# Four edits to the schedule of a hybrid encoder layer: output rows split one at a time, wider value copies, later linear attention groups, the second gate tile before the last norm

## The chip, the cores and the metric

The kernel runs on one core of a Trainium2 chip. The metric is device time in microseconds (us) of one execution, lower is better; the time given for a kernel is the median of its runs.

## What is computed

One layer of a streaming encoder, in float32, on 1024 tokens of width 1024. Cut to what matters:

```
h = rmsnorm(x, ln1);  z = h @ w_in            # columns: pool 256, gla q/k/v/g 4 x 256, gate rank 16,
                                              #          fox q/k/v 3 x 512, forget 8
y_pool = pool_mixer(u)                        # trailing means over 2, 4, 8, 16 tokens, minus identity, per-group linear
y_gla  = gla_mixer(q, k, v, g, a)             # chunked gated linear attention, 4 heads of 64, chunks of 64:
    bcum = cumsum(log_sigmoid(a @ w_a_up + b_a) / 16)            # the decays
    S_t = dec * S_{t-1} + k_in^T v;  o = causal(q k^T) v + q S   # within a chunk, and from the state
    o = rmsnorm(o) * gla_gn * silu(g)
y_fox  = fox_mixer(q, k, v, f)                # causal softmax(q k^T / 8 + F_t - F_s) v, 8 heads of 64,
                                              #   F = cumsum(log_sigmoid(f + b_f))
x = x + concat(y_pool, y_gla, y_fox) @ w_o
h = rmsnorm(x, ln2)
x = x + (silu(h @ w_gate) * (h @ w_up)) @ w_down                 # 22 tiles of 128 hidden columns
out = rmsnorm(x, ln_f)
```

## The kernel before

Every large matmul is done in three: both operands are split into a high part, rounded to TensorE's fp32r format by ScalarE, and a low part, the difference (VectorE or GpSimd), and high x high, high x low and low x high are added in PSUM (`gemm`, `woven`, L139 to L155).

**Memory.** On-chip memory is a set of slots of 128 x 1024 floats. `G` (L50) takes the slot that has been free longest (first in, first out) and `free` gives it back; `R` (L60) takes slots in turn from a small ring: `w` holds split weights (4 slots), `wr` raw weights (2), `p` attention scores (6), `pp` (3), `fb` (2). A tile's first write waits until all that read or wrote the slot's last owner are done, DMAs included. PSUM has eight banks in four groups (L27): `s` 3, `pt` 2, `o` 1, `gm` 2.

**Order.** The program is one straight list of instructions. A planner with a simulated timeline lays out each engine's order when the kernel is built: among what it believes ready it takes what stands first in the program, and it fills gaps with later work, however far down the program. On the chip each engine then follows its list strictly, and waits at an instruction whose inputs or slot are not there. All loads and stores but four go through SP's queue, which waits in order too.

**Stages**, with their rough place in the profile:

- Norm and transposes of x, the gate-rank and linear attention value projection (to 56 us).
- `decays` (L302): logits of the decays, log-sigmoid and running sums for both groups j of two linear attention heads, and for the forget gates F (stored to `Fd`).
- `pool_in`, then the linear attention groups `A = Gla(0)` and `B = Gla(1)` (L660 to L674). Each group has three projections (`keys`, `queries`, `gates`), and small pieces of TensorE work are woven into the projections' matmuls as `smalls`: `turn_keys` (tile pk), `state` (pkv), `within` (pat), `outputs` (po), `turned` (pot), and the pool's matmul (py). What has finished is split into high and low and stored by `keep_mix` (L270) to `mixs`.
- `fox_values(0)` (L517): values of the first two head pairs, eight token blocks, tile psv; each block is copied out as a high and a low part for each of two pairs, four instructions. Its tiles `v` hold one pair and four token blocks each. The last smalls of group B are woven in here.
- `keep_wo` (L279), eight times: a row block of the output weights is loaded, split and stored to `wod`, through three `G` slots.
- Four head pairs: `fox_qk(p)` (tiles zq, zk) and `fox_attend(p)` (L627; scores s, transposes pt, outputs o), which begins with the load of its bias rows `fb` from `Fd`. The values of the last two pairs are made after pair 1. At the end of each pair its tiles are freed (L684 to L695).
- Output projection in two halves of the contraction: `pxa` with row blocks 0 to 3 (L698 to L707), `pxb` with 4 to 7 (L934 to L951), each over eight token blocks; `fetch_wo` and `load_mix` bring the parts back from memory. After `pxb` of a block follows its second norm, `norm2` (L717; transposes n2pt in `pt`).
- SwiGLU, 22 gate tiles: seven products each in the place of eight (`gate_up`, L764, tile m; products are numbered 1 to 7 and come in the order 3, 5, 4, 1, 2, 7, 6, each 12 matmuls). `left` makes left operands hA from the transposed norm, `right`/`make` right operands wr from the weights. Products 3 and 5 need tokens 0 to 511 alone. Then the down projection the same way (tile d), and the last norm.

Around the last block of `pxb`, the first gate tile's first two products are started ahead of the norm:

```python
        if tb == NT - 1:
            for _ in range(2):
                next(first[0])
        SP.dma_start(x3d[tb], xs[tb])
        norm2(tb, xs[tb])
        free(f"xa{tb}")
    free(*[f"wo{k}{h}" for k in range(4, 8) for h in "hl"], "ln2b", *[f"mix{k}_1" for k in range(4, 8)])
    first.append(start(1))
    makes[1](3, 5)
    for _ in range(2):
        next(first[1])
```

The second gate tile is `start(1)`; product 3 goes to a bank of `s`, product 5 to one of `pt`.

Of the kernel before, what the change touches and what calls it, by code (L numbers as in the profile page):

```python
# [10 lines left out]
F32R = mybir.dt.float32r  # L11
I8 = mybir.dt.int8
AF = mybir.ActivationFunctionType
ALU = mybir.AluOpType
# [17 lines left out]
def tile_hybrid_block(ctx: ExitStack, tc, x, w_fv, w_gv, w_zt, w_o, w_gu, w_down, ln, w_pool, w_a3, chans, b_f, consts, out):  # L32
# [36 lines left out]
    def f(ap):  # L69
        return ap.bitcast(F32)  # L70
# [208 lines left out]
    def keep_wo(k):  # L279

        hi, lo = load_g(w_o[k * P:(k + 1) * P, :], f"wos{k}", tag="G")
        SP.dma_start(wod[k, :, 0], f(hi))
        SP.dma_start(wod[k, :, 1], f(lo))
        free(f"wos{k}h", f"wos{k}l")
# [15 lines left out]
    bcs = []  # L300

    def decays():  # L302

        las = []
        for j in range(2):
            la = R(f"la{j}")
            for c in range(2):
                csl = slice(c * 512, c * 512 + 512)
                ps = PS("s", f"pla{j}_{c}")
                PE.matmul(ps, wa[:, j * P:(j + 1) * P], aT[0:48, csl], start=True, stop=True)  # L310
                DVE.tensor_scalar(out=la[:, csl], in0=ps, scalar1=ch[:, 2 + j:3 + j], scalar2=None, op0=ALU.add)
            las.append(la)
        lft = R("lft")
        log_sigmoid([(la, la, R(f"lat{j}", tag="pp")) for j, la in enumerate(las)] + [(fx[0:8], fx[0:8], lft[0:8])])
        for j, la in enumerate(las):
            bc = G(f"bc{j}")
            DVE.tensor_tensor_scan(out=bc, data0=reset, data1=la, initial=0.0, op0=ALU.mult, op1=ALU.add)
            bcs.append(bc)
        ones, Fc = R("ones"), R("Fc")
        DVE.memset(ones[0:8], 1.0)  # L320
        DVE.tensor_tensor_scan(out=Fc[0:8], data0=ones[0:8], data1=fx[0:8], initial=0.0, op0=ALU.mult, op1=ALU.add)
        SP.dma_start(Fd, Fc[0:8])
        free("fx")
# [193 lines left out]
    def fox_values(q, smalls=((),) * NT):  # L517

        V = [[G(f"v{2 * q + j}_{i}", F32R).rearrange("p (t h s e) -> p t h s e", t=4, h=2, s=2) for i in range(2)] for j in range(2)]
        ws = [load_w(w_fv[:, q, i * 1024:(i + 1) * 1024], f"wfv{q}_{i}", eng=POOL) for i in range(2)]  # L520
        for tb in range(NT):
# [3 lines left out]
            for j in range(2):  # L525
                v_ = V[j][tb // 4][:, tb % 4]
                pv = ps[:, 128 * j:128 * j + 128].rearrange("p (h e) -> p h e", h=2)
                ACT.activation(v_[:, :, 0], pv, AF.Copy)
                DVE.tensor_tensor(out=v_[:, :, 1], in0=pv, in1=f(v_[:, :, 0]), op=ALU.subtract)
# [19 lines left out]
    def fox_item(p, a, m, ops, fb, V, Y):  # L549
# [44 lines left out]
        for n in range(m + 1):  # L594
# [10 lines left out]
            for b in range(2):  # L605
                kb = 2 * n + b
                o0 = cut * b
                v_ = V[p % 2][kb // 4][:, kb % 4, a]
# [51 lines left out]
    decays()  # L660
    free("aT", "reset", "wa")
# [3 lines left out]
    A.queries(((), A.turn_keys()))  # L665
    pools = pool_tile(1, us[1]), pool_tile(0, us[0])
    A.gates((A.state(), pools[0] + A.within(0)))
    B = Gla(1)
    B.keys((A.within(1) + A.outputs(0), A.outputs(1) + A.turned(0)))
    B.queries((A.turned(1) + pools[1], B.turn_keys()))  # L670
    free("misc")
    B.gates((B.state(), B.within(0)))
    o_ = [B.outputs(0), B.outputs(1)]
    V = fox_values(0, (B.within(1), o_[0][:1], o_[0][1:], o_[1][:1], o_[1][1:] + B.turned(0), B.turned(1), (), ()))  # L674
    for k in range(8):
        keep_wo(k)
    ops = fox_qk(0)
    free("gv0", "gv1", "attb0", "attb1")
    for p in range(4):
# [4 lines left out]
        done = [f"{n}{p}_{a}" for n in ("q", "k", "kl") for a in range(2)] + [f"v{p}_{i}" for i in range(2)]  # L684
        if p == 1:
            V = fox_values(1)
            free(*[done.pop() for _ in range(2)])
# [248 lines left out]
    for tb in range(NT):  # L936
# [9 lines left out]
        if tb == NT - 1:  # L946
            for _ in range(2):
                next(first[0])
# [3 lines left out]
    free(*[f"wo{k}{h}" for k in range(4, 8) for h in "hl"], "ln2b", *[f"mix{k}_1" for k in range(4, 8)])  # L952
    first.append(start(1))
    makes[1](3, 5)
    for _ in range(2):
        next(first[1])
# [166 lines left out]
```

## Time and profile before

| | us |
|---|---|
| median of 3 runs | 1177.58 (1176.51 to 1179.23) |
| profiled execution | 1175.42 |
| its span, first to last instruction | 1173.7 |
| TensorE matmul busy | 1136.0 |
| VectorE busy | 828.2 |
| ScalarE busy | 536.0 |
| GpSimd busy | 340.4 |

Times in the profile are from the span's start. PE is TensorE's matmuls, PEld its weight loads, DVE VectorE, ACT ScalarE, POOL GpSimd, SP the queue that issues DMAs; a name with q is an engine's queue. A row of a timeline has the start, the busy time, engine, line, operation, tile written and tiles read, form and count, and in brackets the idle time ahead of it and what ended that. A row of the waits has who waited for whom, the sum in us, how often, and the longest. A row of windows has the stretch, its length, each engine's busy time with its count, TensorE's granted clock (1.00 is full speed), the share of the DMA engines and GB/s. Matmuls are pipelined, so the busy time of one overlaps the next.

### The profile page before, as it was taken

The numbers are of one execution on the slowest core, as the hardware profiler recorded it, in microseconds if no ns is written. First come the engines' busy times: TensorE is split into PE (matmuls) and PEld (weight loads), VectorE is DVE, ScalarE is ACT, GpSimd is POOL, SyncE is SP. The second block draws the span as 40 slices with busy tenths as digits, with TensorE's granted clock in tenths as the row PEclk, the third lists the DMA queues.
The fourth block names the chain that finished last, engine by engine and source line by source line (L and its number), as shares of the span: only waits on it lengthen the run. The fifth ranks groups of instructions, "written<-read, shape, count | busy, mean of one in ns | idle before, by whom it ended". The sixth has DMA issues, their size and how long they took to land.

```text
span 1173.7 us, 15953 instructions
## 1 busy us (share of the span) xinstructions
PE 1136.0 (97%) x5928; PEld 958.5 (82%) x5928; DVE 828.2 (71%) x1365; ACT 536.0 (46%) x970; POOL 340.4 (29%) x260
## 2 busy tenths in 40 slices
PE   6999998999999999998999999999999999999996
PEld 5877878889978888886888888888888888888875
DVE  6697364387746866579997767767686685876686
ACT  6454233466654644456453433444344344334345
POOL 2231123343322413210302221022201370660784
PEclk9999999999999999999999999999999999999999
DMA  7121184411203734431323332242314688333233
GB/s 250 37 73 52 59 295 174 176 39 35 91 18 126 305 132 159 173 112 46 117 86 129 101 115 88 101 134 82 135 54 152 224 322 293 103 95 102 86 112 143
DMA packets 57692, 150.45 MB, mean 128 GB/s; under 512 B 5080, under 2 KB 5512, under 8 KB 57616
## 3 DMA queue, kind: packets, MB, share of 16 engines
q1 hardware_dynamic: 57184, 147.87, 36.5%
q0 software_dynamic: 432, 1.57, 0.4%
q8 instruction: 46, 0.75, 0.3%
q14 instruction: 30, 0.25, 0.1%
HBM read 105.09 MB, written 44.34 MB: 127 GB/s over the span
## 4 chain that ended last, share of the span: by engine, by line
PE 76%; DVE 4%; DMA 1%; issue 1%; POOL 1%; ACT 1%; SPq 0%; POOLq 0%; DVEq 0%; ACTq 0%
PE m L774 36%; PE d L1030 15%; PE pxa L144 4%; PE pxb L144 3%; PE o L615 3%; PE pt L601 2%; PE psv L152 2%; PE s L575 1%; PE s L576 1%; PE zq3p L152 1%; PE zq0p L152 1%; PE zq2p L152 1%; PE zk1p L152 1%; PE zk2p L152 1%; PE zk0p L152 1%
## 5 line engine op out<-in xcount | busy, mean ns | idle before, releaser
L774 PE MATMUL m<-hA_0h,wr 128*128 128x512 f32 x616 | 214.7, 391 | 1.2 <-ACT hr L729 1.2
L774 PE MATMUL m<-hA_1h,wr 128*128 128x512 f32 x616 | 214.9, 389 | 0.0
L774 PEld LDWEIGHTS m<-hA_0h,wr 128*128 128x128 f32 x616 | 116.1, 189 | 25.8 <-ACT hr L729 1.6
L774 PEld LDWEIGHTS m<-hA_1h,wr 128*128 128x128 f32 x616 | 115.8, 188 | 24.2
L1030 PE MATMUL d<-lw,ha 128*128 128x512 f32 x308 | 119.9, 389 | 0.9 <-DVE lw L880 0.9
L774 PE MATMUL m<-hA_0l,wr 128*128 128x512 f32 x308 | 120.3, 391 | 0.0
L774 PE MATMUL m<-hA_1l,wr 128*128 128x512 f32 x308 | 119.9, 389 | 0.0
L1030 PE MATMUL d<-hw,ha 128*128 128x512 f32 x308 | 119.3, 389 | 0.0
L1030 PE MATMUL d<-hw,la 128*128 128x512 f32 x308 | 118.4, 389 | 0.0
L756 ACT ACTIVATE wr<-ws 128x512 fp32r<-128x512 f32 x110 | 69.5, 632 | 101.5 <-DVE ws L755 50.1
L826 POOL TENSOR_TENSOR cg<-cu,cu 128x512 f32<-128x512 f32 x11 | 19.7, 1795 | 302.8 <-DVE cu L803 266.7
L757 DVE TENSOR_TENSOR wr<-ws,wr 128x512 fp32r<-128x512 f32 x110 | 76.8, 704 | 20.6 <-ACT wr L756 20.5
L880 DVE TENSOR_TENSOR la<-ra,ha 128x1024 fp32r<-128x1024 f32 (+1 forms) x42 | 57.2, 1368 | 32.0 <-ACT ha L879 24.7
L590 POOL TENSOR_TENSOR pb<-pb,rl 128x128 f32<-128x128 f32 (+3 forms) x32 | 39.0, 1222 | 117.5 <-DVE rl L587 108.9
L872 POOL TENSOR_TENSOR rw<-wd,wd 128x512 f32<-128x512 f32 x33 | 59.0, 1815 | 47.7 <-PE d L1030 47.6
L879 ACT ACTIVATE ha<-ra 128x1024 fp32r<-128x1024 f32 (+1 forms) x42 | 41.3, 987 | 65.6 <-DMA ra<-cd 56.8
L1030 PEld LDWEIGHTS d<-lw,ha 128*128 128x128 f32 x308 | 57.8, 188 | 13.3 <-DVE lw L880 1.3
L604 DVE TENSOR_TENSOR pp<-pt,pp 128x512 fp32r<-128x512 f32 (+1 forms) x80 | 50.2, 631 | 25.7 <-ACT pp L603 25.3
L774 PEld LDWEIGHTS m<-hA_0l,wr 128*128 128x128 f32 x308 | 58.1, 189 | 12.0
L774 PEld LDWEIGHTS m<-hA_1l,wr 128*128 128x128 f32 x308 | 58.0, 188 | 12.0
L1030 PEld LDWEIGHTS d<-hw,la 128*128 128x128 f32 x308 | 57.8, 188 | 12.1
L1030 PEld LDWEIGHTS d<-hw,ha 128*128 128x128 f32 x308 | 57.8, 188 | 11.9
(398 smaller groups left out, 2690.6 us busy)
## 6 DMA issues: line engine op xcount, KB each, us to landing
ra<-cd SPq DMA_DIRECT2D x35, 512.0 KB, 3.9
wu<-in_w_gu_dram SPq DMA_DIRECT2D x22, 512.0 KB, 4.6
wg<-in_w_gu_dram SPq DMA_DIRECT2D x22, 512.0 KB, 3.7
wd<-in_w_down_dram SPq DMA_DIRECT2D x22, 512.0 KB, 6.4
mix<-mixs SPq DMA_DIRECT2D x14, 512.0 KB, 5.3
cd<-cg SPq DMA_DIRECT2D x11, 512.0 KB, 6.3
cd<-cs SPq DMA_DIRECT2D x11, 512.0 KB, 3.4
cd<-cu SPq DMA_DIRECT2D x11, 512.0 KB, 3.3
```

The lines of the kernel that those rows point to most:

```text
L144: PE.matmul(ps, a, b, start=(n == 0), stop=(n == last))
L152: PE.matmul(ps, a, b, start=(i == 0 and n == 0), stop=(i == len(terms) - 1 and n == 2))
L590: POOL.tensor_tensor(out=pb[:, 0:W], in0=pb[:, 0:W], in1=rl[:, 0:1].broadcast_to([P, W]), op=ALU.mult)
L604: DVE.tensor_tensor(out=pp[:, 512:512 + w], in0=pt[:, 0:w], in1=f(pp[:, 0:w]), op=ALU.subtract)
L615: PE.matmul(*args, start=(kb == 0 and n_ == 0), stop=(last and n_ == 1))
L756: ACT.activation(hi, src, AF.Copy)
L757: DVE.tensor_tensor(out=lo, in0=src, in1=f(hi), op=ALU.subtract)
L774: PE.matmul(ps, a, b, start=(n == 0), stop=(n == 11))
L872: POOL.tensor_tensor(out=raw_[:, j * 512:j * 512 + 512], in0=wd[h0, j0 + j][:, e0, :], in1=wd[h1, j0 + j][:, e1, :], op=op)
L879: ACT.activation(hi[:, sl], src, AF.Copy)
L880: DVE.tensor_tensor(out=lo[:, sl], in0=src, in1=f(hi[:, sl]), op=ALU.subtract)
L1030: PE.matmul(banks[t], a[:, o], b[:, ns], start=(j0 + j == 0 and m == 0), stop=(j0 + j == NF // 2 - 1 and m == 2))
```

## The change

Four edits:

1. `keep_wo` holds a row block and its high part in the two slots of the ring `fb`, makes the low part in place, and is called in four pairs between the linear attention projections instead of eight times after `fox_values(0)`.
2. A value tile `v` holds two pairs and two token blocks, so that one copy and one subtraction move a token block where four instructions did. All four tiles are freed after the second of the two pairs, where half of them were freed after each.
3. `decays` is cut into `decay_logits`, `decay_sums(0)`, `decay_sums(1)` and `forget_sums`; the second sum comes after group A's queries, the forget sums after A's gates. The smalls of groups A and B move on by one half projection or more: `turn_keys` from the queries into the gates, and so on, up to token block 6 of `fox_values(0)`.
4. The second gate tile is started before the last norm, and its first two products run there in turn with the first tile's.

```diff
     def keep_wo(k):
-        hi, lo = load_g(w_o[k * P:(k + 1) * P, :], f"wos{k}", tag="G")
+        raw, hi = R(f"wos{k}", tag="fb"), R(f"wosh{k}", F32R, tag="fb")
+        SP.dma_start(raw, w_o[k * P:(k + 1) * P, :])
+        ACT.activation(hi, raw, AF.Copy)
+        DVE.tensor_tensor(out=raw, in0=raw, in1=f(hi), op=ALU.subtract)
         SP.dma_start(wod[k, :, 0], f(hi))
-        SP.dma_start(wod[k, :, 1], f(lo))
-        free(f"wos{k}h", f"wos{k}l")
+        SP.dma_start(wod[k, :, 1], raw)
...
-            la = R(f"la{j}")
+            la = G(f"la{j}")
...
+    def decay_sums(j):
+        la = las[j]
+        log_sigmoid([(la, la, R(f"lat{j}", tag="pp"))])
+        bc = G(f"bc{j}")
+        DVE.tensor_tensor_scan(out=bc, data0=reset, data1=la, initial=0.0, op0=ALU.mult, op1=ALU.add)
+        bcs.append(bc)
+        free(f"la{j}")
+
+    def forget_sums():
+        lft, ones, Fc = (R(n, tag="pp") for n in ("lft", "ones", "Fc"))
+        log_sigmoid([(fx[0:8], fx[0:8], lft[0:8])])
...
     def fox_values(q, smalls=((),) * NT):
-        V = [[G(f"v{2 * q + j}_{i}", F32R).rearrange("p (t h s e) -> p t h s e", t=4, h=2, s=2) for i in range(2)] for j in range(2)]
+        V = [G(f"v{q}_{i}", F32R).rearrange("p (t j h s e) -> p t j h s e", t=2, j=2, h=2, s=2) for i in range(4)]
...
-            for j in range(2):
-                v_ = V[j][tb // 4][:, tb % 4]
-                pv = ps[:, 128 * j:128 * j + 128].rearrange("p (h e) -> p h e", h=2)
-                ACT.activation(v_[:, :, 0], pv, AF.Copy)
-                DVE.tensor_tensor(out=v_[:, :, 1], in0=pv, in1=f(v_[:, :, 0]), op=ALU.subtract)
+            v_ = V[tb // 2][:, tb % 2]
+            pv = ps[:, 0:256].rearrange("p (j h e) -> p j h e", j=2, h=2)
+            ACT.activation(v_[:, :, :, 0], pv, AF.Copy)
+            DVE.tensor_tensor(out=v_[:, :, :, 1], in0=pv, in1=f(v_[:, :, :, 0]), op=ALU.subtract)
...
-    decays()
-    free("aT", "reset", "wa")
+    decay_logits()
+    decay_sums(0)
+    free("aT", "wa")
     us = [pool_in(j) for j in range(2)]
     A = Gla(0)
     A.keys()
-    A.queries(((), A.turn_keys()))
+    A.queries()
+    decay_sums(1)
+    free("reset")
     pools = pool_tile(1, us[1]), pool_tile(0, us[0])
-    A.gates((A.state(), pools[0] + A.within(0)))
+    A.gates((A.turn_keys(), A.state()))
+    keep_wo(0)
+    keep_wo(1)
+    forget_sums()
     B = Gla(1)
-    B.keys((A.within(1) + A.outputs(0), A.outputs(1) + A.turned(0)))
-    B.queries((A.turned(1) + pools[1], B.turn_keys()))
+    B.keys((A.within(0) + pools[0], A.within(1) + A.outputs(0)))
+    keep_wo(2)
+    keep_wo(3)
+    B.queries((A.outputs(1) + A.turned(0), A.turned(1) + pools[1]))
     free("misc")
-    B.gates((B.state(), B.within(0)))
+    keep_wo(4)
+    keep_wo(5)
+    B.gates((B.turn_keys(), B.state()))
+    keep_wo(6)
+    keep_wo(7)
     o_ = [B.outputs(0), B.outputs(1)]
-    V = fox_values(0, (B.within(1), o_[0][:1], o_[0][1:], o_[1][:1], o_[1][1:] + B.turned(0), B.turned(1), (), ()))
-    for k in range(8):
-        keep_wo(k)
+    V = fox_values(0, (B.within(0), B.within(1), o_[0][:1], o_[0][1:], o_[1][:1], o_[1][1:] + B.turned(0), B.turned(1), ()))
...
-        done = [f"{n}{p}_{a}" for n in ("q", "k", "kl") for a in range(2)] + [f"v{p}_{i}" for i in range(2)]
+        done = [f"{n}{p}_{a}" for n in ("q", "k", "kl") for a in range(2)] + [f"v{p // 2}_{i}" for i in range(4) if p % 2]
         if p == 1:
             V = fox_values(1)
-            free(*[done.pop() for _ in range(2)])
+            free(*[done.pop() for _ in range(4)])
...
         if tb == NT - 1:
+            free(*[f"wo{k}{h}" for k in range(4, 8) for h in "hl"], *[f"mix{k}_1" for k in range(4, 8)])
+            first.append(start(1))
+            makes[1](3, 5)
             for _ in range(2):
-                next(first[0])
+                for g_ in first:
+                    next(g_)
         SP.dma_start(x3d[tb], xs[tb])
         norm2(tb, xs[tb])
         free(f"xa{tb}")
-    free(*[f"wo{k}{h}" for k in range(4, 8) for h in "hl"], "ln2b", *[f"mix{k}_1" for k in range(4, 8)])
-    first.append(start(1))
-    makes[1](3, 5)
-    for _ in range(2):
-        next(first[1])
+    free("ln2b")
```

More of the change, by code (lines that the diff above doesn't have):

```diff
@@ L299, in tile_hybrid_block, with decay_logits @@
     DVE.memset(e3(reset)[:, :, 0:1], 0.0)
-    bcs = []
-    def decays():
-        las = []
+    las, bcs = [], []
+    def decay_logits():
         for j in range(2):
-            la = R(f"la{j}")
+            la = G(f"la{j}")
             for c in range(2):
@@ L312, in decays @@
             las.append(la)
[L313 to L319, printed above, removed]
+    def decay_sums(j):
[8 more added lines that the diff above has]
+        log_sigmoid([(fx[0:8], fx[0:8], lft[0:8])])
         DVE.memset(ones[0:8], 1.0)
@@ L607, in fox_item @@
                 o0 = cut * b
-                v_ = V[p % 2][kb // 4][:, kb % 4, a]
+                v_ = V[kb // 2][:, kb % 2, p % 2, a]
                 ph = pp[:, 256 * b:512 - o0] if b else pp[:, 0:256]
```

## The prediction

> **What bounds the kernel now.** I read the page first, then TensorE's waits, then windows as long as the clock's own steps, then the engines' timelines around each wait.
>
> ```profile
> span 1173.7 us, 15953 instructions
> PE 1136.0 (97%) x5928; PEld 958.5 (82%) x5928; DVE 828.2 (71%) x1365; ACT 536.0 (46%) x970; POOL 340.4 (29%) x260
> ```
>
> TensorE is the bound, and the change leaves its work as it is. So the time can only move through idle TensorE and through TensorE at a lower clock: 1173.7 - 1136.0 = 37.7 us are idle in all. The profiled execution took 1175.4 us (its span and 1.7 us around it), 2.2 us under the median of 1177.6. My sum is a difference, and I take it off both.
>
> ```profile
> PE n2pt L727 <- DVE n2sq L722: 3.5, 1, 3.5
> PE zq0p L152 <- DVE v L529: 3.5, 1, 3.5
> PE zq3p L152 <- DVE kl L544: 2.5, 1, 2.5
> PE pk L375 <- DVE d L351: 2.1, 1, 2.1
> PE psv L152 <- DVE v L529: 1.5, 1, 1.5
> ```
>
> The change is aimed at four of these five waits; the third (zq3p) it leaves alone or makes longer. A wait costs more than its length, as the windows show:
>
> ```profile
> 172.83:176.24 3.41, 1.87 (x30) 1.70 (x29) 2.60 (x6) 1.74 (x7) 0.00 (x0) 1.00 0.70 284
> 176.24:179.65 3.41, 3.41 (x19) 3.41 (x18) 0.38 (x2) 0.00 (x0) 1.64 (x1) 0.50 0.11 43
> 200.14:203.55 3.41, 0.96 (x4) 0.83 (x5) 2.89 (x4) 1.14 (x2) 3.41 (x2) 1.00 0.85 339
> 203.55:206.96 3.41, 3.41 (x10) 2.63 (x9) 0.00 (x0) 0.00 (x0) 1.02 (x1) 0.50 0.98 292
> 538.06:541.47 3.41, 1.07 (x8) 0.85 (x8) 3.41 (x6) 1.47 (x5) 0.00 (x0) 1.00 0.00 0
> 541.47:544.88 3.41, 3.27 (x8) 2.62 (x9) 3.41 (x7) 3.41 (x9) 0.00 (x0) 0.50 0.00 0
> ```
>
> The columns are the window, its length, then the busy time of TensorE, its weight loads, VectorE, ScalarE and GpSimd, then the granted clock. Where TensorE is busy for 1.87 us or less of a 3.41 us window, the next window runs at 0.50, and half of 3.41 us, 1.7 us, of work is lost once more. So the psv wait costs 1.5 + 1.7 = 3.2 us, and the zq0p wait 3.5 + 1.7 = 5.2 us.
>
> The Trainium skill ("TensorE: Matmul & The Clock Gate", "HAM oscillation — how this bites in real kernels") asks for no idle gaps of TensorE above about 3.4 us. Here the trace differs: the 1.5 us psv wait was enough. By the page's rule removing that wait would bring 1.5 us in place of 3.2, and the sum would be 1.7 us smaller; I go by the windows.
>
> **Rows of the output projection, later groups, wider copies.**
>
> ```profile
> 173.24 1.23 DVE L119 TENSOR_TENSOR wos6l<-wos6r,wos6h 128x1024 fp32r<-128x1024 f32 x1 [2.84 <-ACT wos6h L118]
> 174.38 1.12 DVE L529 TENSOR_TENSOR v<-psv,v 128x128 fp32r<-128x128 f32 x4
> 199.75 2.58 DVE L119 TENSOR_TENSOR wos1l<-wos1r,wos1h 128x1024 fp32r<-128x1024 f32 x1 [1.77 <-ACT wos1h L118]
> 202.26 0.47 DVE L529 TENSOR_TENSOR v<-psv,v 128x128 fp32r<-128x128 f32 x2
> 197.72 1.06 ACT L118 ACTIVATE zq0h<-zq0r 128x1024 fp32r<-128x1024 f32 x1 [1.03 <-PE psv L152]
> 198.91 2.35 POOL L119 TENSOR_TENSOR zq0l<-zq0r,zq0h 128x1024 fp32r<-128x1024 f32 x1 [7.11 <-issue]
> ```
>
> In both places VectorE splits a row block of the output weights (wos) while the value copies that would free TensorE's bank (v) stand behind it. After the change the eight splits come earlier, among the linear attention stages, so the psv wait and its slow window go: 3.2 us (from 1.5, if another split or reduction stands there, to 3.2). At zq0p the bank will be free, but the weights are not: their high part is split only when the values' last use of that ring slot is over (197.72), and GpSimd ends the low part at 198.91 + 2.35 = 201.26. The old wait began at 202.59 - 3.5 = 199.1. So up to 201.26 - 199.1, some 2 us, of wait is left; the planner may fill it with products of the high part. I take 1.9 us left and no slow window, a gain of 5.2 - 1.9 = 3.3 us (1.6 if the slow window stays, 5.2 if the gap is filled).
>
> The pk wait (2.1 us) is TensorE at the key transposes, with VectorE late by the decay sums and the pool. The transposes move from the second half of the query projection to the gate projection, some 24 large matmuls later; of the work in front of VectorE the second decay sum becomes less urgent too. I take all 2.1 us (0 if VectorE's queue is reordered against it).
>
> ```profile
> L528 ACT ACTIVATE v<-psv x32: 255/277/280, 173.1 to 313.2; 128x128 fp32r<-128x128 f32 x32
> 43.81 0.39 ACT L184 ACTIVATE hT<-n1s 128x256 fp32r<-128x256 f32 x1
> ```
>
> The wider copies replace two of 0.28 us by one of 0.39, sixteen times on ScalarE and the like on VectorE: 16 x 0.17 = 2.7 us an engine. Neither engine is the bound there and the bank's release is counted above, so by itself this is 0; without TensorE's cover it would be 2.7 at most.
>
> The one-at-a-time split puts a row block and its high part in the ring of two slots that the bias rows of attention (fb) use next. So a block's load waits for both stores of the block before, on SP's queue, with later weight loads behind it.
>
> ```profile
> wos2r<-in_w_o_dram SPq DMA_DIRECT2D x1, 512.0 KB, 4.9
> wod<-wos7l SPq DMA_DIRECT2D x1, 512.0 KB, 4.8
> 98.79 0.71 PE L152 MATMUL zgg0p<-hT,zgg0h 128*128 128x512 f32 x2
> 230.09 0.29 DVE L580 CUSTOM_DVE_ANT_0 pb<-s,fb 128x128 f32<-128x128 f32 x1
> ```
>
> One block takes 4.9 (load) + 1.06 + 1.23 (splits) + 4.8 (store) = 12.0 us, eight 96 us. From the first gate projection, 98.79, they end at 195, and a bias row is wanted at 230.09. About 30 us hide it: 0.
>
> **The second gate tile.**
>
> ```profile
> 531.99 0.60 ACT L780 ACTIVATE cu<-m 128x512 f32<-128x512 f32 x1 [1.28 <-PE m L774]
> 536.33 0.39 PE L774 MATMUL m<-hA_1h,wr 128*128 128x512 f32 x1
> 538.82 1.27 DVE L722 SCALAR_TENSOR_TENSOR n2sq<-xa,n_r,ln2b 128x1024 f32<-128x1024 f32 x1
> 541.61 0.80 PE L774 MATMUL m<-hA_0h,wr 128*128 128x512 f32 x1 [0.31 <-ACT hr L729]
> 545.98 1.32 PE L774 MATMUL m<-hA_0h,wr 128*128 128x512 f32 x5
> 549.76 0.60 ACT L785 ACTIVATE cg<-m 128x512 f32<-128x512 f32 x1 [0.57 <-DVE cu L784]
> ```
>
> The planner had already put the second tile's product 3 ahead of the norm (its drain is the row at 531.99), so of the two steps only product 5 moves. Today it runs from 541.61 to 545.98, after the last norm's transposes, most of it in the slow window (it is drained up to 549.76). Moved, its 12 matmuls fill the wait from 536.6 to about 539.3. The norm's row at 538.82 stays where it is, ending at 540.09. The second half of the transposes now needs the bank that product 5 uses: an add and a copy after 540.1 (0.6 us each, by the copy at 531.99) free it at 541.3. Transposes with their copies take 1.5 us today (540.1 to 541.6), and a split of the left operand is one more copy; these some 2 us start the next product at about 543.4, not 545.98: 2.5 us. VectorE is busy for all of 3.41 us in both windows there, and could take it all back (0); with no slow window after it is 2.5 + 1.7 = 4.2.
>
> **What the slots cost.** Free slots are handed out first in, first out, so a new value layout shifts who follows whom. Following the list through the code, the values' first half is now given back only after two head pairs. Three places feel it.
>
> ```profile
> 425.07 0.52 SPq L647 DMA_DIRECT2D mix<-mixs  x1
> 436.42 0.32 SPq L275 DMA_DIRECT2D mixs<-mh  x1
> 441.05 2.35 SPq L704 DMA_DIRECT2D xa<-in_x_dram  x2
> mix<-mixs SPq DMA_DIRECT2D x14, 512.0 KB, 5.3
> 434.29 0.39 PE L144 MATMUL pxa<-wo0h,mix 128*128 128x512 f32 x1
> 434.29:446.40 12.11, 7.62 (x33) 5.78 (x31) 1.00 0.87 308
> ```
>
> The fourth mix tile of the second token half, loaded at 425.07, takes a value slot today. After, no value slot is free there, and it takes the slot of the third pair's high part, whose store is issued at 436.42 and landed by 441.05, where the load that follows it today is issued. The mix tile then lands at 441.05 + 5.3 = 446.35. The last row is the projection's own matmuls in the 12.11 us from its fifth block on: 33 in 7.62 us, 0.23 each; the other 4.49 us are attention and the rest. Without the fourth tile only 3 of 4 row blocks of two banks can run, 18 matmuls, 4.15 us. TensorE stands for 12.11 - 4.49 - 4.15 = 3.5 us. Nothing covers it: the other banks are taken.
>
> ```profile
> 467.00 0.36 SPq L289 DMA_DIRECT2D wo6h<-wod  x1
> wo6h<-wod SPq DMA_DIRECT2D x1, 512.0 KB, 7.6
> 350.69 1.28 DVE L544 TENSOR_TENSOR kl<-zk2p,k 64x512 fp32r<-64x512 f32 x2 [0.61 <-PE o L615]
> ```
>
> At the second half of the output weights five of eight tiles (wo6h among them) wait today for the first half to end; after, seven do. wo6h, issued third of them, took 7.6 us, so 2.5 us a tile and 5.1 us for two more. They may also land side by side, and attention is left to run: between 0 and 5.1 I take the middle, 2.5 us.
>
> At zq3p the third pair's low key part waits for the second pair's values (350.69). After, the high part does too, one copy more in the chain, like one of the two in that row: 0.6 us (0 to 1.3).
>
> **The sum.** Gains 3.2 + 3.3 + 2.1 + 2.5 = 11.1 us, losses 3.5 + 2.5 + 0.6 = 6.6 us: 4.5 us faster, 1175.4 to 1170.9 in the profile and 1177.6 to 1173.1 as median. Its own range is 1170 to 1176.
>
> **Rivals.**
> - The new waits are absorbed: the planner places attention's last pair into the hole, or the mix tile comes in time. Then only the 0.6 us loss stays: 1177.6 - 10.5 = 1167.1; with a filled zq0p gap and no slow window at 541 down to 1163.5. For it: attention has priority over the projection. Against: 3.41 us windows at 538 show how full VectorE gets beside it. 24%.
> - Slower: the projection's late slots win. With a mix landing like wo6h's, 7.6 in place of 5.3, the hole is 5.8 us; two of its windows pass the half and bring two slow ones, 3.4; the weights cost the full 5.1. Losses 0.6 + 5.8 + 3.4 + 5.1 = 14.9 against 11.1: 1177.6 + 3.8 = 1181.4. It decides from 10.5 us of idle between 434 and 480 on. 15%.
> - Nothing in the end: VectorE takes back the 2.5 us after 541, and the 1.9 us at zq0p make a slow window after all (1.7). 4.5 - 4.2 = 0.3: 1177.3. 12%.
> - The split of the output rows is late: above (230.09 - 98.79 - 4.9) / 8 = 15.8 us a block, the first bias row is late, by eight times the excess: at 17 us some 10 us, 1183. 4%.
>
> **Chances.** My forecast has 45%, of which about a ninth lies within 0.2% (2.4 us, about what a measurement of this kernel can tell from no change) of 1177.6. Faster is 0.40 + 0.24 = 0.64, same 0.05 + 0.12 = 0.17, slower 0.15 + 0.04 = 0.19. The range 1164.5 to 1182 leaves out the tail of the first rival, the late splits, and the upper part of the slower one.
>
> **What would show it.** Right: TensorE's waits for v at psv and for d at pk are gone, zq0p waits for its low weights for 2 us or less, and n2pt for under 1.5; product 5 of the second gate tile is drained before the last norm's transposes; a mix load is issued right after the store of the third pair's high part, and a new wait of TensorE for it stands in the output projection; row blocks are stored before 200 us. Wrong: no such wait between 434 and 480 (then the first rival), the bias rows of the first pair loaded after 230 us, or a slow window in the places where I took one away.

## The result and the profile after

The change makes the kernel slower: 1187.93 us (1186.70 to 1189.82) against 1177.10 us (1176.51 to 1179.23), a ratio of 1.0097 with a 95% interval of 1.0085 to 1.0109, 10.8 us. My forecast was 1173.1, and the range ended at 1182.

From here on the columns are those of the front part. First the page after, then TensorE's waits after; the change shifts line numbers by 5 to 15.

```profile
span 1188.1 us, 15915 instructions
PE 1141.0 (96%) x5928; PEld 960.2 (81%) x5928; DVE 822.0 (69%) x1349; ACT 533.5 (45%) x956; POOL 345.4 (29%) x260
```

```profile
PE zgq0p L152 <- ACT gk L356: 8.5, 1, 8.5
PE pxb L144 <- DMA mix<-mixs: 2.7, 1, 2.7
PE zq3p L152 <- DVE kl L549: 2.2, 1, 2.2
PE m L789 <- ACT hA_0h L918: 2.0, 1, 2.0
PE n2pt L742 <- DVE n2sq L737: 2.0, 1, 2.0
PE s L580 <- POOL k L551: 1.8, 1, 1.8
...
PE pxa L144 <- DMA mix<-mixs: 1.3, 1, 1.3
...
PE zq0p L152 <- DVE v L534: 0.5, 1, 0.5
```

The waits for pk and psv are gone, zq0p waits 0.5 us in place of 3.5, and the norm's wait (n2pt for n2sq) is 2.0 in place of 3.5: what the change was aimed at moved the right way. But there is one wait of 8.5 us, in linear attention's first query projection, where before there was none, and several of 1 to 3 us in attention, the output projection and the second gate tile.

To see what each stage lost, take for every matmul the time to the start of the next one beyond the median step of its form, and add this up by stage (us; it holds waits and slow clock alike):

| kernel | group A (zgk0 to zgk1) | group B, values, zq0 | pairs 0 to 3 (to zk3) | pair 3, projection (up to the last blocks' norms) | the next 30 us |
|---|---|---|---|---|---|
| before | 4.8 | 17.0 | 7.6 | 3.1 | 7.3 |
| changed | 11.9 | 11.8 | 10.5 | 11.6 | 9.3 |
| difference | +7.1 | -5.2 | +2.9 | +8.5 | +2.0 |
| forecast | -2.1 | -6.5 | +0.6 | +6.0 | -2.5 |

The differences add to 15.3; outside these stages 1.9 came back. (The profiled executions lie 14.4 us apart, the medians 10.8; so 1.0 us of the former is placed nowhere.)

**Group A.** The next four blocks are rows of the timelines after (GpSimd, ScalarE, VectorE) and the windows there.

```profile
78.88 10.45 POOL L345 TENSOR_TENSOR d<-bc 128x1024 f32<-128x1024 f32 x1 [41.24 <-DVE bc L319]
116.33 1.94 POOL L346 TENSOR_TENSOR d<-bc 128x1024 f32<-128x1024 f32 x1 [6.16 <-DVE pd L508]
```

```profile
79.92 0.58 ACT L356 ACTIVATE gk<-zgk0p 128x512 f32<-128x512 f32 x1
89.36 1.06 ACT L347 ACTIVATE d<-d 128x1024 f32<-128x1024 f32 x1 [8.86 <-POOL d L345]
...
97.04 0.58 ACT L356 ACTIVATE gk<-zgk0p 128x512 f32<-128x512 f32 x1
```

```profile
78.95 0.91 DVE L326 MEMSET ones<- 8x1024 f32 x1
79.79 1.15 DVE L119 TENSOR_TENSOR zgq0l<-zgq0r,zgq0h 128x1024 fp32r<-128x1024 f32 x1
80.87 2.27 DVE L319 TENSOR_TENSOR_SCAN bc<-reset,la 128x1024 f32<-128x1024 f32 x1
83.06 1.19 DVE L495 TENSOR_TENSOR pa<-u 128x1023 f32<-128x1023 f32 x1
84.18 2.27 DVE L327 TENSOR_TENSOR_SCAN Fc<-ones,fx 8x1024 f32<-8x1024 f32 x1
86.38 1.19 DVE L284 TENSOR_TENSOR wos<-wos,wosh 128x1024 f32<-128x1024 f32 x1
87.50 0.13 DVE L494 COPY pa<-u 128x1 f32<-128x1 f32 x1
87.56 2.84 DVE L495 TENSOR_TENSOR pa<-u 128x1023 f32<-128x1023 f32 x1
```

```profile
89.08:92.49 3.41, 0.09 (x1) 0.00 (x0) 3.41 (x3) 1.44 (x3) 3.41 (x4) 1.00 0.51 174
92.49:95.91 3.42, 0.00 (x0) 0.00 (x0) 0.85 (x1) 3.42 (x4) 2.61 (x1) 0.50 0.12 49
...
99.32:102.73 3.41, 3.41 (x9) 2.63 (x9) 3.40 (x5) 0.00 (x0) 0.00 (x0) 0.50 0.92 250
```

GpSimd's subtraction takes 10.45 us where the same form takes 1.94 at 116.33. Through all of it VectorE runs without a gap, at its usual durations, until the small copy at 87.50; the operation behind that copy then takes 2.84 us, so there GpSimd got in. ScalarE's exponential (89.36) waits for GpSimd, and in its queue behind it, after six more instructions, stands the copy of the key projection's second half (97.04), which empties the PSUM bank that TensorE needs. Three windows at half clock follow, 92.49 to 102.73. Three operations of VectorE's run stand there because of the change: the forget gate's memset (78.95) and scan (84.18), and a row split (86.38).

**Other places.** Stores and loads from 442 to 488 us, to be read beside the SP rows of before:

```profile
442.24 0.33 SPq L275 DMA_DIRECT2D mixs<-mh  x1
...
446.57 5.49 SPq L652 DMA_DIRECT2D mix<-mixs  x2
...
473.10 0.33 SPq L291 DMA_DIRECT2D wo7h<-wod  x1
...
478.22 8.77 SPq L652 DMA_DIRECT2D mix<-mixs  x2
```

As forecast, a mix tile follows the store of the third pair's high part, and seven weight tiles instead of five wait for the first half. The first hole is small (pxa 1.3 us). The larger one is a mix load behind the seven on SP's queue: pxb 2.7 us, with a slow window.

```profile
352.01 1.07 ACT L548 ACTIVATE k<-zk2p 64x512 fp32r<-64x512 f32 x2
...
354.06 1.08 ACT L548 ACTIVATE k<-zk2p 64x512 fp32r<-64x512 f32 x2
```

The third pair's four key copies all wait for the second pair's values. Before, two of them ran earlier, at 336.60 and 344.58:

```profile
336.60 0.59 ACT L543 ACTIVATE k<-zk2p 64x512 fp32r<-64x512 f32 x1 [1.43 <-PE zk2p L152]
344.58 0.57 ACT L543 ACTIVATE k<-zk2p 64x512 fp32r<-64x512 f32 x1
```

### The profile page after: what moved, and what is told of

Read it like the earlier page. It is cut to its first block, busy times and chain, and to the rows that moved or that the text cites. A ratio compares the mean times of both kernels' runs of the same rounds, so it can differ in the third digit from the quotient of the medians.

```text
span 1188.1 us, 15915 instructions
## 1 busy us (share of the span) xinstructions
PE 1141.0 (96%) x5928; PEld 960.2 (81%) x5928; DVE 822.0 (69%) x1349; ACT 533.5 (45%) x956; POOL 345.4 (29%) x260
## 4 chain that ended last, share of the span: by engine, by line
PE 60%; DVE 3%; POOL 3%; DMA 2%; issue 1%; ACT 1%; POOLq 0%; DVEq 0%; ACTq 0%
PE m L789 35%; PE d L1045 13%; PE pxb L144 4%; PE pxa L144 3%; POOL rw L887 2%; PE zq3p L152 1%; PE pt L606 1%; PE o L620 1%; PE zk3p L152 1%; POOL c L1008 1%; DMA mix<-mixs 1%; PE s L580 1%; DMA wo5h<-wod 1%; PE s L581 1%; PE n2pt L742 0%
## 5 line engine op out<-in xcount | busy, mean ns | idle before, releaser
L589 ACT ACTIVATE pb<-pb,mn 128x128 f32<-128x128 f32 (+3 forms) x64 | 49.4, 773 | 52.9 <-DVE mn L585 52.3
L1045 PEld LDWEIGHTS d<-lw,ha 128*128 128x128 f32 x308 | 57.8, 188 | 11.9
```

Source lines behind the costliest of these rows:

```text
L589: ACT.activation(pb[:, 0:W], pb[:, 0:W], AF.Exp, bias=mn[:, 0:1], scale=-1.0, accum_out=l[:, i:i + 1])
L1045: PE.matmul(banks[t], a[:, o], b[:, ns], start=(j0 + j == 0 and m == 0), stop=(j0 + j == NF // 2 - 1 and m == 2))
```

## The experiments

My first theory: the loss comes from GpSimd held off in group A and from the value slots; the split of the rows is a gain. Each difference below is between the median of a kernel and that of the kernel before, run in the same session; the 95% interval of the ratio stands in brackets.

### Each part alone

**Rows** (edit 1 on the kernel before, called at the change's places in the old groups):

```diff
-        hi, lo = load_g(w_o[k * P:(k + 1) * P, :], f"wos{k}", tag="G")
+        raw, hi = R(f"wos{k}", tag="fb"), R(f"wosh{k}", F32R, tag="fb")
...
```

> The kernel before with the split of the output weights' rows alone taken from the change (two buffers of the ring fb, one block at a time, called at the places of the change). Theory (the loss comes from GpSimd held off at 78.9 us by a queue of VectorE work and from the value slots given back later; the split of the rows itself is a gain): the waits of TensorE at psv and zq0p shrink, no stall of over 3 us before 110 us; 3 to 6 us faster, 1171.5 to 1174.5. Rival (the early row blocks are what delays GpSimd's subtractions and the loads): a stall of some 8 us with slow windows after it at about 89 us; 3 us slower or more, 1180 to 1185.

Measured 1168.89, 7.0 us faster (0.9914 to 0.9956). The second stage of the table falls from 17.0 to 10.4, and group A has no long stall (6.1). A gain, somewhat larger than expected.

**Groups** (edit 3 alone; `keep_wo` as before, after the values):

```diff
-    decays()
+    decay_logits()
+    decay_sums(0)
...
```

> The kernel before with the linear attention's later groups alone (decay sums one at a time, forget sums after them, groups one product later); rows, values and gate tile as before. Theory: the forget gate's scan now stands on VectorE right behind the first decay sum, so that VectorE has no break after it and GpSimd's subtraction of two SBUF tensors waits; the stall at 88.8 us comes in this kernel too, 5 us or more with slow windows, while pk (2.1 us) goes: 4 to 8 us slower, 1181 to 1186. Rival (the row splits make the stall): no stall, pk gone, 2 us faster, 1175.5.

Measured 1174.40, 1.4 us faster (0.9973 to 0.9997). The stall is there without any row split (GpSimd's subtraction 8.22 us, TensorE's wait 4.7), but my time was wrong: the groups' gains outweigh it. The pk and psv waits are gone and zq0p waits 1.8 us, so the second stage falls from 17.0 to 12.9. These rows of GpSimd and VectorE show how GpSimd's subtraction ends there:

```profile
71.97 8.22 POOL L343 TENSOR_TENSOR d<-bc 128x1024 f32<-128x1024 f32 x1 [36.15 <-DVE bc L317]
```

```profile
76.23 2.27 DVE L317 TENSOR_TENSOR_SCAN bc<-reset,la 128x1024 f32<-128x1024 f32 x1
78.43 3.91 DVE L325 TENSOR_TENSOR_SCAN Fc<-ones,fx 8x1024 f32<-8x1024 f32 x1
```

The second scan takes 3.91 us where it takes 2.27 in the changed kernel: here GpSimd got in between two full scans, after some 8.22 - 1.94 = 6.3 us, with no small operation between them.

**Values** (edit 2 alone):

```diff
-        V = [[G(f"v{2 * q + j}_{i}", F32R).rearrange("p (t h s e) -> p t h s e", t=4, h=2, s=2) for i in range(2)] for j in range(2)]
+        V = [G(f"v{q}_{i}", F32R).rearrange("p (t j h s e) -> p t j h s e", t=2, j=2, h=2, s=2) for i in range(4)]
...
```

> The kernel before with the wider value copies and their four slots alone. Theory: the slots come back after two head pairs, so TensorE waits at the third pair's keys (2 to 3 us more), at the output projection for mix tiles and weights (some 9 us): 1184 to 1189, nearly nothing gained at psv. Rival (the waits in the projection come from transfers of the earlier stages or from the gate tile): within 2 us of the kernel before, 1176 to 1179.

Measured 1186.60, 10.8 us slower (1.0058 to 1.0099). Pairs 0 to 3 lose 10.2 (7.6 before) and the projection 11.6 (3.1), as in the changed kernel.

**Gate tile** (edit 4 alone):

```diff
...
+            first.append(start(1))
+            makes[1](3, 5)
             for _ in range(2):
-                next(first[0])
+                for g_ in first:
+                    next(g_)
...
```

> The kernel before with the second gate tile begun ahead of the last norm alone. My forecast's step: 2.5 us faster, 1175.1, up to 4.2 with the slow window gone. Theory after the trace: the last norm's small GpSimd operation is held off by back-to-back VectorE work, and the splits of the left operand run late, so that the wait for the norm is only moved: from 1 us faster to 2 us slower, 1176.5 to 1179.5.

Measured 1178.27, 2.4 us slower (1.0009 to 1.0028): my forecast's 2.5 us gain is a loss of the same size. TensorE does not wait longer between 520 and 560 us (4.4 us in all, before 4.7); what grew there is the stretch at half clock, 10.24 us from 541.33 on, in place of 3.41. The mean granted clock of the ten runs is 0.987 to 0.990, with a median of 0.988, against 0.991 for the kernel before, so this was not the profiled run alone.

The four add to -7.0 - 1.4 + 10.8 + 2.4 = +4.8 us, where the whole change costs 10.8. Six are an interaction.

### Rows and groups together

**Rows and groups**, old values and old gate start (both diffs above):

> Rows and later groups together, with the old value layout and the old gate start. Theory (VectorE's splits of the rows and the forget scan keep GpSimd out together): the wait before zgq0p is 8 us or more with slow windows after it, against 4.7 us with the groups alone; 1173 to 1177, worse than the rows alone (1168.9). Rival (the effects add): 1166.5 to 1168.5, better than the rows alone.

Measured 1176.62, no different from the kernel before (+1.3 us, 0.9997 to 1.0023), where the two alone add to -8.4. So an interaction is here, 9.7 us, and the table's measure shows two parts of it. In group A, TensorE's wait is 8.7 us and the stage loses 11.9 (rows alone 6.1, groups alone 7.2, before 4.8): some 3.4 us more than the two would add to. In the second stage, rows and groups take away the same waits, so their gains don't add: it loses 10.4 with the rows, 12.9 with the groups and 12.5 with both (before 17.0), some 6.2 us of gain counted twice.

**Changed kernel with the old values:**

> The changed kernel with the old value layout (two copies of 128x128, slots given back pair by pair); rows, groups and gate tile as changed. Theory (each of the parts keeps its own price, and the split rows and the later groups make the GpSimd wait of 8.5 us longer than the groups alone do): 10 us faster than the changed kernel, 1176 to 1179. Rival (the single effects add up without any interaction, -7.0 -1.4 +2.4 beside the kernel before): 1170 to 1172.

Measured 1177.34, +2.1 us (1.0004 to 1.0022), as the theory had it. The values cost 10.8 - 2.1 = 8.7 us in the changed kernel.

**Group 0's subtractions on VectorE**, in the changed kernel and in rows and groups:

```diff
-            POOL.tensor_tensor(out=e3(d2), in0=b3[:, :, 63:64] ...
+            eng = POOL if j else DVE
+            eng.tensor_tensor(out=e3(d2), in0=b3[:, :, 63:64] ...
...
```

> The changed kernel with the first group's two subtractions (the decay differences of group 0) on VectorE in place of GpSimd; all else as changed. Theory (GpSimd's subtraction is held off for as long as VectorE runs operations of two SBUF inputs without a break): with nothing left for GpSimd to do there, the wait of 8.5 us and the three half-clock windows at 92 us go, VectorE has 2.4 us more: 1187.9 falls by 8 to 12 us, to 1176 to 1180. Rival (VectorE's queue is too long there, whoever subtracts): the wait stays at 5 us or more, 1184 to 1188.

> Rows and later groups, old value layout, old gate start, and group 0's two subtractions on VectorE. Theory: the wait before zgq0p goes and the gains of the groups (pk 2.1 us, psv) stay: 1163 to 1167, the fastest kernel so far. Rival: a wait of 4 us or more stays before zgq0p, 1168 or above.

Measured 1188.26, +13.0 us (1.0086 to 1.0116), and 1174.32, -1.0 us (0.9976 to 0.9996). The theory failed as stated: the wait stays, 7.8 us in the first. Its GpSimd and ScalarE rows tell why:

```profile
81.99 8.38 POOL L346 TENSOR_TENSOR d<-bc 128x1024 f32<-128x1024 f32 x1 [4.20 <-DVE bc L319]
```

```profile
90.40 2.00 ACT L348 ACTIVATE d<-d 128x1024 f32<-128x1024 f32 x2 [8.23 <-POOL d L346]
```

Group 1's subtraction had taken the place of group 0's: held off in the same run of VectorE, with ScalarE waiting for it ahead of the same copies. Either VectorE's longer queue is itself to blame, or this subtraction has to go too.

**Both groups' subtractions on VectorE**, in rows and groups, in the changed kernel, and with the rows alone:

```diff
-            POOL.tensor_tensor(out=e3(d2), in0=b3[:, :, 63:64] ...
+            DVE.tensor_tensor(out=e3(d2), in0=b3[:, :, 63:64] ...
...
-            POOL.tensor_tensor(out=e3(d1), in0=b3, in1=b3[:, :, 31:32] ...
+            DVE.tensor_tensor(out=e3(d1), in0=b3, in1=b3[:, :, 31:32] ...
```

> Rows and later groups (old value layout, old gate start) with the subtractions of both groups on VectorE, so that GpSimd has nothing to do before ScalarE's copies of the key projection. Theory (the held-off GpSimd operation delays ScalarE, whose copy of the key projection would free TensorE's bank; with group 0 alone moved, group 1's subtraction took its place): the wait of 8 us before zgq0p goes, or falls to 2 us or less, though VectorE has 4.8 us more work; 1176.6 falls to 1164 to 1168. Rival (VectorE's queue itself delays ScalarE): a wait of 5 us or more stays, 1172 or above.

> The changed kernel with the subtractions of both groups on VectorE, all else as changed. Theory (GpSimd held off costs the whole change what it costs rows and groups without the rest, 8.5 us): the wait of 8.5 us before zgq0p falls under 2 us, 1187.9 falls to 1177 to 1181; what is left above the kernel before belongs to the value slots and the gate tile. Rival (VectorE's longer queue costs as much again in the changed kernel): 1183 or above.

> The rows alone (old groups, values, gate start) with the subtractions of both groups on VectorE. Theory (in the kernel before, GpSimd and VectorE take turns there, each operation standing for the other, and the key transposes wait 1.9 us for it): the pk wait shrinks, from 0 to 2 us faster than the rows alone (1168.9), 1166.5 to 1169. Rival (VectorE is the later engine there, and 4.8 us more on it delay the transposes): 1170 to 1173.

Measured 1168.09, -7.7 us (0.9914 to 0.9947); 1180.47, +3.4 us (1.0019 to 1.0040); 1166.55, -10.5 us (0.9894 to 0.9926). TensorE's wait in the first of them:

```profile
PE zgq0p L152 <- ACT gk L356: 1.3, 1, 1.3
```

The wait of 8.7 is 1.3, though VectorE does more. In the changed kernel it is 0.6, worth 10.8 - 3.4 = 7.4 us. And with the rows alone the pk wait (1.9 us there) goes as well, a gain of 3.6 us where I expected 0 to 2; that is the fastest kernel here, 10.5 us ahead of the kernel before. Rows and groups together, with the subtractions moved, are not ahead of it: beside the rows the groups bring no gain that could be seen. In the rows with the subtractions moved, one of them costs VectorE 1.22 us:

```profile
75.62 1.22 DVE L342 TENSOR_TENSOR d<-bc 128x1024 f32<-128x1024 f32 x1
```

**Forget sums first**, in rows and groups, with the subtractions on GpSimd and on VectorE:

```diff
     decay_logits()
+    forget_sums()
     decay_sums(0)
...
-    forget_sums()
```

> Rows and later groups (old value layout, old gate start) with the forget gate's sums ahead of the first decay sum, as in the kernel before; the subtractions stay on GpSimd. Theory (GpSimd waits until VectorE leaves its run of operations of two SBUF inputs; a memset and a scan less in that run make it shorter, and they run earlier instead): GpSimd's first subtraction takes 4 to 8 us in place of 10.45, the wait of TensorE falls from 8.5 to between 2 and 6 us; 1169 to 1174. Rival (the forget scan has no part in it): 1176 or above.

> Rows and later groups with both subtractions on VectorE and the forget gate's sums ahead of the first decay sum. Theory (VectorE's run after the first decay sum is 3.2 us shorter, so that the 1.3 us left before zgq0p go): 1165.5 to 1168, against 1168.1 without. Rival (the forget sums only move the work ahead of the decay sum, which comes later by as much, and the wait for the state at pkv grows as it did with the subtractions on GpSimd): 1168 to 1171.

Measured 1173.68, -2.1 us (0.9974 to 0.9995): GpSimd's subtraction 6.13 us, TensorE's wait 2.1, but a new one of 3.6 at pkv. And 1169.64, -7.4 us (0.9916 to 0.9945): nothing gained over 1168.09; group A loses 0.6 in place of 2.2 in the table, the next stage 15.4 in place of 13.7. The rival holds there: the loss moved on to the next stage.

### What lets GpSimd in

Two twins of rows and groups have three more operations of one column, which nothing uses, in VectorE's queue; in one twin they are copies, in the other the column is added to itself (`DVE.tensor_tensor(out=br, in0=bc[:, 0:1], in1=bc[:, 0:1], op=ALU.add)`). Two stand behind the decay sums, the third behind the split of zgq0:

```diff
         bcs.append(bc)
+        br = cst.tile([P, 1], F32, name=f"br{j}")
+        DVE.tensor_copy(br, bc[:, 0:1])
...
```

> Rows and later groups (subtractions on GpSimd), with three copies of one column (128x1, nothing uses them) added to VectorE; the first of them falls between the pool's first sum and the forget gate's scan, inside the run that keeps GpSimd out, all other orders unchanged. Theory (GpSimd gets in where VectorE runs a small operation of one input, as at the copy at 87.67 of rows and groups): GpSimd's first subtraction ends after that copy, some 7.1 us in place of 10.45, TensorE's wait of 8.5 us falls by some 3.4 us, and with a slow window or two less the time falls by 3 to 7 us, from 1176.6 to 1170 to 1174, although the kernel does more. Rival (VectorE's run has to end, or its queue's length decides): 10.4 us and 8.5 us stay, 1176 to 1178.

> The same three additions in the same places as operations of two inputs (the column added to itself, 128x1). Theory by the number of SBUF inputs: an operation of two inputs holds GpSimd's reads off, however short, so nothing changes: 10.4 us, a wait of 8.5 us, 1175.5 to 1178. Rival (any short operation leaves a gap in VectorE's queue in which GpSimd gets in): as with the copies, some 7.1 us and 1170 to 1174.

Measured 1172.87, -3.2 us (0.9960 to 0.9983), and 1173.47, -2.6 us (0.9969 to 0.9990), against +1.3 without. GpSimd's row with copies, then VectorE's rows from the small operation on, with copies and with additions:

```profile
77.49 7.13 POOL L350 TENSOR_TENSOR d<-bc 128x1024 f32<-128x1024 f32 x1 [41.50 <-DVE bc L322]
```

```profile
82.79 0.14 DVE L325 COPY br<-bc 128x1 f32<-128x1 f32 x1
82.85 3.91 DVE L332 TENSOR_TENSOR_SCAN Fc<-ones,fx 8x1024 f32<-8x1024 f32 x1
```

```profile
83.54 1.84 DVE L325 TENSOR_TENSOR br<-bc 128x1 f32<-128x1 f32 x1
85.31 2.27 DVE L332 TENSOR_TENSOR_SCAN Fc<-ones,fx 8x1024 f32<-8x1024 f32 x1
```

GpSimd's operation is 7.13 us long in both, as expected of the copies. TensorE's wait falls from 8.7 to 6.3 and 6.7 us, somewhat less than the 3.4 expected, and two windows run at half clock in place of three. Three useless operations make the kernel some 4 us faster: a one-column operation in the run is enough to let GpSimd in. It is not needed, as the groups alone showed. My theory that the number of inputs decides is wrong: with copies the scan behind them stands for GpSimd (3.91 in place of 2.27), with additions the small operation itself does (1.84).

### Slots and gate tile

**Value slots given back late**, copies as before:

```diff
-        done = [f"{n}{p}_{a}" for n in ("q", "k", "kl") for a in range(2)] + [f"v{p}_{i}" for i in range(2)]
+        done = [f"{n}{p}_{a}" for n in ("q", "k", "kl") for a in range(2)] + [f"v{p - 1 + j}_{i}" for j in range(2) for i in range(2) if p % 2]
...
-            free(*[done.pop() for _ in range(2)])
+            free(*[done.pop() for _ in range(4)])
```

> The kernel before with one line changed: the value slots of a head pair are given back only when the pair after it is done too; the value copies stay as they were. Theory (the loss of the wide copies is the slots given back two pairs later and nothing else): the same waits at the third pair's keys and in the output projection as with the wide copies, 1184 to 1189. Rival (the wide copies themselves, or the order of the four slots, make the loss): within 3 us of the kernel before, 1174 to 1179.

Measured 1184.95, +9.1 us (1.0059 to 1.0089), with the waits of the wide copies (in the waits: s for k 1.8, wo5h 2.3, pxa for mix 1.1). So the late slots alone cost 9.1 us, and the whole values edit 10.8, with intervals that overlap; the wide copies bring no gain that could be seen.

**Gate tile without the last root.** The last row block's norm leaves out the inverse root that GpSimd takes, so that VectorE doesn't wait for it there:

```diff
-        DVE.scalar_tensor_tensor(out=sq, in0=x2, scalar=r[:, 0:1], ...
+        DVE.scalar_tensor_tensor(out=sq, in0=x2, scalar=(ss if tb == NT - 1 else r)[:, 0:1], ...
...
```

> The kernel before with the gate tile's early start, and the last row block's norm scaled by its mean square as it comes from ScalarE, in place of the inverse root that GpSimd takes of it (left out: that factor, in this one row block). Theory (GpSimd's small operation is held off for 2.1 us by VectorE's run, and the norm with it): the wait of TensorE for the norm falls from 2.0 us to under 0.5, and the kernel is 2 to 4 us faster than with the gate start alone (1178.3), 1174 to 1176. Rival (the order of the splits of the left operand sets the end): the wait moves to those splits, 1177 to 1179.

Measured 1178.29, +2.5 us (1.0008 to 1.0027), no different from the gate tile alone. GpSimd's small operation is held off there too (2.11 us, before 0.82), but the norm's wait fell only from 2.0 to 1.4, with VectorE busy without a gap in front of it. The profiles don't settle more: this one has one slow window less at the norm and one more at 96.47, where the code is the same.

**Half the gate edit** (operands made ahead of the norm, products after it):

```diff
...
+            first.append(start(1))
+            makes[1](3, 5)
             for _ in range(2):
                 next(first[0])
...
-    first.append(start(1))
-    makes[1](3, 5)
```

> The kernel before with only half of the gate edit: the freed buffers, the second tile's loads and the making of its operands 3 and 5 stand ahead of the last norm, but its two products are asked for after it, as before. Theory (VectorE's and ScalarE's splits of the operands pulled ahead of the norm make the loss): as slow as with the whole gate edit, 1177 to 1179.5, and the splits of the left operand wait behind the norm as there. Rival (product 5 itself, which takes a bank that the norm's transposes need, makes it): as the kernel before, 1174.5 to 1176.5.

Measured 1180.27, +3.2 us (1.0010 to 1.0036). Its wait and VectorE's rows:

```profile
PE n2pt L727 <- DVE n2sq L722: 5.7, 1, 5.7
```

```profile
540.83 0.68 DVE L757 TENSOR_TENSOR wr<-wg,wr 128x512 fp32r<-128x512 f32 x1
...
542.03 1.27 DVE L722 SCALAR_TENSOR_TENSOR n2sq<-xa,n_r,ln2b 128x1024 f32<-128x1024 f32 x1
```

The second tile's right operands (wr, ws) now stand ahead of the norm's row, which comes at 542.03, 4.7 us after the start of the last matmul ahead of it (538.82 before, 2.5 us after). The theory holds, though the time lies just above its range: making the operands earlier is enough for the loss. Here it is a longer wait (5.7 us in place of 3.5) and 6.83 us of half clock in place of 3.41; with product 5 in the gap it was half clock alone. What product 5 gives back, if anything, lies within the two intervals.

## Why the prediction was wrong

**Rows and values at TensorE's bank (6.5 us): right.** Measured 5.2 in the changed kernel, 6.6 in the rows alone. Summing the halved windows was right too: without them 3.4 us less would have been due. The rest that I left at zq0p, 1.9 us for the low weights, is there in the groups alone (1.8) and in rows and groups (1.6); in the changed kernel 0.5 us was left, for the value copy.

**"I take all 2.1 us (0 if VectorE's queue is reordered against it)", the pk term: the failed step.** The wait went, but I thought of VectorE's queue and not of GpSimd's, and let the bound end at zero. Two rows of GpSimd in the kernel before, which the prediction leaves out, show the two engines standing for one another there (1.94 us is the time of one alone):

```profile
73.51 2.79 POOL L339 TENSOR_TENSOR d<-bc 128x1024 f32<-128x1024 f32 x1 [23.07 <-DVE bc L317]
76.26 3.92 POOL L340 TENSOR_TENSOR d<-bc 128x1024 f32<-128x1024 f32 x1
```

The change adds a memset, a scan and a split to VectorE's run there, and GpSimd's subtraction ahead of ScalarE's copies took 10.45 us. Group A came out at +7.1 for -2.1, and moving the subtractions took 7.4 us out of the changed kernel. The Trainium skill ("SBUF — State Buffer", "Who interferes with whom") says that a VectorE operation with two SBUF inputs and a GpSimd operation that reads SBUF block one another, the second to start waiting until the first is done. The trace agrees that they block one another, but not on how long: by that rule GpSimd's wait is at most one operation of VectorE, 2.27 us here; it was held off through the whole run, some 8.7 us. The page would have been reason enough to follow GpSimd's queue too.

**"About 30 us hide it: 0", the split of the rows: failed in its place.** I let the blocks begin at 98.79. In the trace the planner had begun before 45 us, and a block took 8.6 us, not 12:

```profile
43.62 0.33 SPq L285 DMA_DIRECT2D wod<-wosh  x1
...
52.21 0.32 SPq L285 DMA_DIRECT2D wod<-wosh  x1
...
123.30 0.32 SPq L286 DMA_DIRECT2D wod<-wos  x1
126.43 1.20 SPq L636 DMA_DIRECT2D fb<-Fd  x2
```

The bias rows are loaded at 126.43, 100 us early. But an early split is one more operation of VectorE in group A (86.38), and there rows and groups meet: GpSimd's subtraction takes 10.45 us with both and 8.22 with the groups alone, TensorE's wait 8.7 and 4.7.

**Slots (6.6 us): mechanism right, size too small.** Pairs and projection lost 11.4 together. At the third pair I counted one copy more (0.6) where two copies more waited, and a second slow window followed (2.9). How much of the 2.9 is the copies' own stays open: the groups alone, which leave the pairs' code as it was, also had two slow windows there (6.83 us from 349.33 on) and lost 9.7, 2.1 more than before. In the projection I placed the loss at the first half (3.5) and the weights (2.5); the largest single wait was another, the mix load behind seven weights on SP's queue (2.7 us and a slow window), which I had not followed. The slots alone, in the kernel before, cost 9.1 us.

**Second gate tile (2.5 us gain): "The norm's row at 538.82 stays where it is" failed.** I moved product 5 and not what feeds it: the operands that move with it are VectorE's, and the norm waits behind them (539.70 with the gate tile alone, 542.03 with the operands alone). The one slow window there became three with the gate tile alone and two in the changed kernel.

**Rivals.** The slower one named the right place (projection) and its losses; its 10.5 us of idle was not reached (8.5 us more than before, waits and slow clock together), and the largest wait, 8.5 us at zgq0p, was in none of my cases. Of my marks for right, three failed: the norm's wait was 2.0 us, not under 1.5; the second tile's product 5 ended ahead of the last norm's transposes (553.55) but was drained behind the first of them (its copy by ScalarE started at 554.76); and zq0p waited 0.5 us for a value copy, not for its low weights. Of those for wrong none came true, while the time missed the range: a new wait in a place that I had counted as a gain was on no list.

## What to carry to other kernels

Before work is added to VectorE, look for GpSimd operations that fall into the run it makes, and for what waits for them in the in-order queues (ScalarE's copies out of PSUM above all): here 2 us became 10. When a step is moved ahead of a deadline, move in thought all that feeds it on the engines that the deadline needs. And time the parts of a change one by one: here one part and a small repair (10.5 us faster) were worth more than all four together (10.8 us slower), and two parts that take away the same waits gave that gain only once.

## What the runs showed of the hardware

- GpSimd's operation of 1.94 us took up to 10.45 us while VectorE ran six operations back to back at their usual lengths. It got in at a small operation of one column, with one input or two; but with the groups alone it got in between two full scans, and in the kernel before the two engines took turns (2.79, 3.92 us). What decides between turns and being held off stays open.
- A window of 3.41 us with TensorE busy for 1.71 us was not followed by half clock after 549.88, where one of 1.87 us was in the kernel before:

```profile
549.88:553.30 3.42, 1.71 (x8) 1.09 (x6) 3.42 (x5) 1.20 (x2) 1.73 (x2) 1.00 0.00 0
553.30:556.71 3.41, 1.28 (x8) 0.84 (x8) 3.32 (x7) 2.02 (x6) 0.00 (x0) 1.00 0.01 2
556.71:560.12 3.41, 2.53 (x6) 1.66 (x6) 3.41 (x6) 3.41 (x8) 0.00 (x0) 0.50 0.00 0
```

  So busy time in a window is not all that decides, and the prediction's rule (1.87 us or less) does not hold as stated.
- The same wait can cost one slow window or two. The last norm's wait of 3.5 us, with the same code around it, was followed by 3.41 us of half clock in the kernel before, in rows and groups and in the rows with the subtractions moved, and by 6.83 us in the rows alone, the groups alone and the values alone. That is 1.7 us of difference that no edit at that place made; where the wait falls on the grid of windows may decide it, which is not tested.
